# Fourth chunk of three later feed-forward parts by 7 products instead of 8, with its token sums formed at the head

## The chip, the cores and the metric

One core of one Trainium2 chip runs the whole kernel. The metric is the device time of one execution in microseconds (us), as the median of several runs. A profiled execution gives the trace from which all durations here are read.

## What is computed

Two layers of a hybrid block on 512 tokens of width 1024, in float32. Each layer is feed-forward, token mixing, feed-forward, with a layer norm behind each:

```python
def _swiglu(x, w1, w2):
    gt, up = jnp.split(x @ w1, 2, axis=-1)
    return (jax.nn.silu(gt) * up) @ w2

for l in range(DEPTH):          # DEPTH = 2, D_FF = 2816
    x = _layer_norm(DN_ALPHA * x + 0.5 * _swiglu(x, ffn1_w1[l], ffn1_w2[l]), ...)
    mix = _token_mix(x, ...)
    x = _layer_norm(DN_ALPHA * x + mix, ...)
    x = _layer_norm(DN_ALPHA * x + 0.5 * _swiglu(x, ffn2_w1[l], ffn2_w2[l]), ...)
```

So there are four feed-forward parts. This change concerns the products `x @ w1` of parts two, three and four.

## The kernel before

Every float32 operand is split into a high part, rounded to the type that TensorE multiplies (`hi`, `xh`, `th`; made by ScalarE), and the rest (`lo`, `xl`, `tl`; made by VectorE as operand minus high part). One product of two matrices is then three matmuls: high by high, high by rest, rest by high. Wherever below "product" stands for one 128x128 weight block against tokens, its three matmuls are counted singly.

A feed-forward part (`ffn`, L576) walks over 22 chunks of w1; chunk f is 128 gate columns and 128 up columns. There are two ways to do a chunk:

- Plain (`proj`, L186): gate and up, each 8 blocks of the inner dimension by 3 matmuls over all 512 tokens: 48 matmuls of 512 columns. With halves of weights and tokens as blocks of a 2 by 2 matrix these are 8 block products.
- By 7 products (`strassen`, L630, after Strassen and Winograd): 7 block products of 4 blocks by 3 matmuls over 256 tokens: 84 matmuls of 256 columns. It needs sums of the weights (`Pair.sums`, L522: four VectorE subtractions and additions into two `ws` tiles), the splits of `ug`, `u1`, `u2` and `ud` (`Pair.hi`, L532, high part on ScalarE, `lo` on VectorE at L544), and sums of the tokens (`token_sums`, L554: x put together from `xh` and `xl` in four VectorE instructions at L566, four subtractions at L570, split at L572 and L573 into `th` and `tl`). The token sums are formed once per part.

The head of a part runs in this order. Chunks 0 and 1 are done by `staged` (L464) with weights that the part before has loaded; each of their four results (`pj`) is done for 256 tokens first and for the other 256 behind. Their weights (`hi`, `lo`) lie in a pool `nx`, which is given back (`done_prev`, L685) when the matmuls have been issued. Then pools are opened in that memory: `fb` with `hb` (the last four chunks' results), `fa` with `ha` (one tile of 18 chunks' results, 36 KB in each partition, L691) and, on the other side of memory, `w1p` with the tiles for sums. These pools have `reuse_waits="tile"`: a tile in memory that was used before waits for those who used it before. Then `evac` (L584) makes silu(gate) times up of chunks 0 and 1, first ScalarE (L586, from PSUM to a place in `ha`), then VectorE (L587). Chunks 2 and 3 are plain. Beside them VectorE forms the token sums, evacuates chunk 2, and prepares chunk 4's weights. From chunk 4 to chunk 21 all are done by 7 products: `strassen(f, cur, ahead)` with the next chunk's sums and splits put between its products as `slots`.

In the last three parts TensorE, GpSimd, ScalarE and VectorE run their instructions in the order of the code (`in_order`, L256, entered at L681 since `l or which` holds). In the first part this begins at chunk 4 only. PSUM has eight banks, given in turn by a ring (`ps`, L81); a result tile waits until the bank's last user is done. Weight splits are put into pools in turn (`unit`, L144): a counter `more.n` picks the pool.

Names used below: `pj` results of chunks 0 and 1; `pg`, `pu` and `pv` results of gate, up and the third bank of a chunk; `ha` the tile of chunk results; `ws` sums of weights; `dl` the rest of `ud`.

Of the kernel before, what the change touches and what calls it, by code (L numbers as in the profile page):

```python
# [9 lines left out]
F32 = mybir.dt.float32  # L10
F32R = mybir.dt.float32r
BF = mybir.dt.bfloat16
AF = mybir.ActivationFunctionType
OP = mybir.AluOpType
# [4 lines left out]
P = 128  # L19
S, D, F = 512, 1024, 2816  # L20
KD, KF, NB = D // P, F // P, S // P
# [43 lines left out]
def body(tc, a, out, depth=DEPTH):  # L65
    nc = tc.nc
# [12 lines left out]
    ring = [0]  # L79

    def ps(tag=None, name="ps", shape=(P, 512)):  # L81
        if tag is None:
            tag = PS_ALL[ring[0] % 8]
            ring[0] += 1
        return psp.tile(list(shape), F32, name=name, tag=tag, bufs=PS_TAGS[tag])
# [22 lines left out]
    xh = xtp.tile([P, KD, S], F32R, name="xh")  # L108
    xl = xtp.tile([P, KD, S], F32R, name="xl")
# [16 lines left out]
    def wraw():  # L126
        pl, n = raws[0]
        raws.rotate(-1)
        return pl.tile([P, KD, P], F32, name="raw", tag="raw", bufs=n)

    more = K()
# [24 lines left out]
    def wsplit(raw, n=KD, step=None):  # L156
        hi, lo = unit()
        step = step or n
        for i in range(0, n, step):
            c = slice(i, i + step)  # L160
            nc.scalar.activation(hi[:, c], raw[:, c], AF.Copy)  # L161
            nc.vector.tensor_tensor(lo[:, c], raw[:, c], hi[:, c].bitcast(F32), op=OP.subtract)  # L162
        return hi, lo

    def wcols(w, c0, step=None):

        r = wraw()
        nc.sync.dma_start(r, w.rearrange("(k p) f -> p k f", p=P)[:, :, c0:c0 + P])
        return wsplit(r, step=step)
# [6 lines left out]
    def mm3(o, w, k, vh, vl, first, last):  # L176
        hi, lo = w
        if lo is None:
            nc.tensor.matmul(o[0:64], hi[:, k, 0:64], vh, start=first, stop=False)
            nc.tensor.matmul(o[0:64], hi[:, k, 0:64], vl, start=False, stop=last)  # L180
            return
        nc.tensor.matmul(o, hi[:, k], vh, start=first, stop=False)  # L182
        nc.tensor.matmul(o, hi[:, k], vl, start=False, stop=False)  # L183
        nc.tensor.matmul(o, lo[:, k], vh, start=False, stop=last)  # L184

    def proj(o, w, n=slice(0, S), ks=range(KD)):  # L186
        for k in ks:
            mm3(o[:, n], w, k, xh[:, k, n], xl[:, k, n], k == 0, k == KD - 1)
# [67 lines left out]
    def in_order():  # L256
        m = tc.manual_schedule(engines={PE, POOL, mybir.EngineType.Activation, mybir.EngineType.DVE})
        m.__enter__()
        return m
# [252 lines left out]
    class Pair:  # L512
# [34 lines left out]
        def all(u):  # L547
# [3 lines left out]
                u.hi(n)()  # L551
            return u

    def token_sums(st):  # L554


        x = st.ha[:, 10:18]
        th, tl = (st.w1p.tile([P, 4, 4, 256], F32R, name=n) for n in ("th", "tl"))
        t = [y[:, i:i + 2].rearrange("p a (b s) -> p (a b) s", b=2) for y, i in
             ((st.hb, 0), (st.hb, 2), (st.ha, 6), (st.ha, 8))]  # L560
        tt = nc.vector.tensor_tensor
        nc.gpsimd.tensor_copy(pace, st.ha[:, 0, 0:1])
        nc.gpsimd.memset(one, 1.0)
        for i in range(0, KD, 2):
            c = slice(i, i + 2)
            nc.vector.scalar_tensor_tensor(x[:, c], xh[:, c].bitcast(F32), one, xl[:, c].bitcast(F32), op0=OP.mult,  # L566
                                           op1=OP.add)
        p_, q, r_, s_ = x[:, 0:4, 0:256], x[:, 0:4, 256:512], x[:, 4:8, 0:256], x[:, 4:8, 256:512]
        for i, u, v in ((0, q, p_), (1, s_, t[0]), (2, s_, q), (3, r_, t[1])):
            tt(t[i], u, v, op=OP.subtract)  # L570
        for i in range(4):
            nc.scalar.activation(th[:, i], t[i], AF.Copy)  # L572
            tt(tl[:, i], t[i], th[:, i].bitcast(F32), op=OP.subtract)  # L573
        st.t = [(th[:, i], tl[:, i]) for i in range(4)]

    def ffn(l, w1, w2, which, xap, xa, wts, pend, done_prev, last, nxt, ts, mid=()):  # L576


        st = K()
# [4 lines left out]
        def evac(f, pg, pu, t=None):  # L584
            t = st.w1p.tile([P, S], F32, name="v", tag="v", bufs=2) if t is None else t
            nc.scalar.activation(t, pg, AF.Silu)  # L586
            nc.vector.tensor_tensor(hpart(f), t, pu, op=OP.mult)  # L587
# [3 lines left out]
        def parts(hi, lo, x):  # L591
            nc.scalar.activation(hi, x, AF.Copy)  # L592
            nc.vector.tensor_tensor(lo, x, hi.bitcast(F32), op=OP.subtract)
# [36 lines left out]
        def strassen(f, u, nxt_, slots=None):  # L630


            if slots is None:
                slots = [nxt_.sums, lambda: (nxt_.hi("ug")(), late.append(nxt_.hi("u1"))),
                         lambda: (late.pop()(), late.append(nxt_.hi("u2"))),
                         lambda: (late.pop()(), late.append(nxt_.hi("ud")))]
            late = []
            t1, t2, t3, t4 = st.t
            ga, pa, pb = ps(name="pg"), ps(name="pu"), ps(name="pv")
            p_, r_, s_ = [(xh[:, k:k + 4, c], xl[:, k:k + 4, c]) for k, c in ((0, H1), (4, H1), (4, H2))]  # L640

            def prod(o, w, k0, x, first=True):
                for k in range(4):
                    hi, lo = w[0][:, k0 + k], w[1][:, k0 + k]
                    vh, vl = x[0][:, k], x[1][:, k]
                    for i, (wx, vx) in enumerate(((hi, vh), (hi, vl), (lo, vh))):
                        nc.tensor.matmul(o, wx, vx, start=first and k == 0 and i == 0, stop=k == 3 and i == 2,  # L647
                                         skip_group_check=True)

            tt = nc.vector.tensor_tensor  # L650
            for g in st.tail:
                g()
            slots[0]()
            prod(ga[:, H1], u.ug, 0, p_)
            prod(ga[:, H2], u.u1, 0, t1, False)
            sn = st.w1p.tile([P, S], F32, name="sn", tag="sn", bufs=2)
            nc.scalar.activation(sn, ga, AF.Copy)
            slots[1]()
            prod(pa[:, H1], u.u1, 4, t2)
            prod(pa[:, H2], u.u2, 0, t3, False)  # L660
            v = st.w1p.tile([P, S], F32, name="v", tag="v", bufs=2)
            h = hpart(f)
            tt(v[:, H1], pa[:, H1], sn[:, H1], op=OP.add)
            tt(v[:, H2], pa[:, H2], v[:, H1], op=OP.add)
            tt(h[:, H2], sn[:, H2], v[:, H2], op=OP.add)
            slots[2]()
            prod(pb[:, H1], u.ud, 0, t4)
            tt(h[:, H1], pb[:, H1], v[:, H2], op=OP.add)
            slots[3]()
            prod(ga[:, H1], u.ug, 4, r_, False)  # L670
            prod(ga[:, H2], u.u2, 4, s_, False)

            def add():
                tt(ga[:, H2], ga[:, H2], v[:, H1], op=OP.add)

            def silu():
                nc.scalar.activation(v, ga, AF.Silu)

            st.tail = [add, silu] + late + [lambda: tt(h, v, h, op=OP.mult)]

        order = in_order() if l or which else None  # L681
        pts = staged(wts, pend, mid)
# [9 lines left out]
        st.w1p = nx.w1 = pool("w1p", side="right", reuse_waits="tile")  # L692
        more.n = 4
        more_raws(st.lnp, 1)
        ws = [(wcols(w1, f * P), wcols(w1, F + f * P)) for f in (2, 3)]
        for f in (2, 3):
            evac(f - 2, *pts[2 * f - 4:2 * f - 2], st.ha[:, f + 2])
        pps = []
        for w in ws:
            pps.append((ps(name="pg"), ps(name="pu")))  # L700
            for o, x in zip(pps[-1], w):
                proj(o, x)
        token_sums(st)
        evac(2, *pps[0])
        cur = Pair(w1, 4).all()
        evac(3, *pps[1])
        st.tail = []
        ahead = Pair(w1, 5)
        order = order or in_order()
        for f in range(4, KF):  # L710
            for i in range(2 if f % 3 == 0 else 1):
                sums_step(hpart(f - 2))
# [1 line left out]
            if f == KF - 1:  # L714
                w = [wt.tile([P, KD, P], F32R, name=n, tag=n, bufs=3).rearrange("p (a b) c -> p a (b c)", a=4)
                     for n in ("hi", "lo")]
                v, sn = (st.w1p.tile([P, 2, 256], F32, name=n, tag=n, bufs=2) for n in ("v", "sn"))
# [6 lines left out]
            cur, ahead = ahead, Pair(w1, f + 2) if f + 2 < KF else None  # L724
        v, sn = (st.w1p.tile([P, 2, 256], F32, name=n, tag=n, bufs=2) for n in ("v", "sn"))
        w = [st.w1p.tile([P, 4, 256], F32R, name="ws", tag="ws", bufs=2) for _ in range(2)]
# [5 lines left out]
        def lo(u, r):  # L732
            nc.vector.tensor_tensor(u[1], r, u[0].bitcast(F32), op=OP.subtract)
# [1105 lines left out]
    w = xl[:, KD - 1, 256:512].bitcast(BF)  # L1839
    nc.vector.memset(w, 1.0)  # L1840
    o = ps("po", "warm")
# [155 lines left out]
```

## Time and profile before

| | |
|---|---|
| median of 3 runs | 2423.96 us (2423.51 to 2423.97) |
| the profiled execution | 2423.59 us |
| its span, first to last instruction | 2421.9 us |
| TensorE (PE) busy | 2408.2 us, 99% |
| VectorE (DVE) busy | 1947.0 us, 80% |
| ScalarE (ACT) busy | 1228.6 us, 51% |
| GpSimd (POOL) busy | 488.2 us, 20% |

The profiled execution lies 1.7 us above its span; that rest lies outside the instructions. A row of the timeline gives start and length in us, the engine, the line of the code, the operation with what it writes and reads, and in brackets how long the engine was idle before it and for whom it waited. Matmuls overlap: a matmul's length is longer than the distance to the next one's start, and it is the distance that adds up. VectorE instructions overlap by some hundredths too.

### The profile page before, as it was taken

Reading aid. Unit: us, or ns where it says so; the run is one execution under the profiler, and the core shown is the slowest. Engines: PE = TensorE matmul, PEld = TensorE weight load, DVE = VectorE, ACT = ScalarE, POOL = GpSimd, SP = SyncE. Lnnn points to the kernel's source line nnn. Section 1 sums busy time; section 2 is a strip of 40 time slices with the busy share of each in tenths; the row PEclk is TensorE's granted clock in tenths of the full one; section 3 lists DMA queues with packets and bytes.
Section 4 is the critical chain, followed back from the end, with each engine's and each line's share of the span. In section 5 each row is a group of like instructions: output and inputs, shape, how many; then the busy total and the mean of one; then the engine's idle time right before and its main releaser. Section 6 shows DMA issues by size and latency. Waiting matters only on the chain.

```text
span 2421.9 us, 41995 instructions
## 1 busy us (share of the span) xinstructions
PE 2408.2 (99%) x15952; PEld 2156.7 (89%) x15952; DVE 1947.0 (80%) x3782; ACT 1228.6 (51%) x2336; POOL 488.2 (20%) x684
## 2 busy tenths in 40 slices
PE   9999999999999999999999999999999999999998
PEld 8999887888889889998899998878888898899987
DVE  6899985687688669999879999666776885799997
ACT  4444645577544334445544446455766443344463
POOL 4232402144410002114000004022443100000040
PEclk9999999999999999999999999999999999999999
DMA  7888754666483536887533347546765735233373
GB/s 208 228 224 216 258 154 138 175 158 157 118 196 96 188 100 166 210 210 243 184 106 105 105 131 250 153 134 168 164 145 119 195 105 183 79 104 106 106 240 121
DMA packets 422586, 390.09 MB, mean 161 GB/s; under 512 B 20472, under 2 KB 352392, under 8 KB 422384
## 3 DMA queue, kind: packets, MB, share of 16 engines
q1 hardware_dynamic: 385792, 287.00, 39.8%
q0 software_dynamic: 36592, 100.41, 17.3%
q8 instruction: 126, 2.06, 0.3%
q14 instruction: 76, 0.62, 0.1%
HBM read 360.02 MB, written 93.38 MB: 187 GB/s over the span
## 4 chain that ended last, share of the span: by engine, by line
PE 99%; DMA 0%; issue 0%; ACT 0%; DVE 0%; DVEq 0%; POOLq 0%; SPq 0%; POOL 0%; ACTq 0%
PE acc L331 18%; PE pg L647 17%; PE pu L647 9%; PE pj L182 6%; PE gate L1657 6%; PE pj L183 6%; PE pj L184 6%; PE pv L647 4%; PE brp L184 2%; PE brp L182 2%; PE brp L183 2%; PE sN L1258 2%; PE ptN L1300 1%; PE po L1319 1%; PE acc L197 1%; PE acc L196 1%
## 5 line engine op out<-in xcount | busy, mean ns | idle before, releaser
L162 DVE TENSOR_TENSOR lo<-raw,hi 128x1024 fp32r<-128x1024 f32 (+2 forms) x186 | 216.5, 1182 | 86.0 <-ACT hi L161 85.1
L182 PE MATMUL pj<-xh,hi 128*128 128x512 f32 (+1 forms) x720 | 267.2, 371 | 0.6 <-ACT hi L161 0.6
L184 PE MATMUL pj<-xh,lo 128*128 128x512 f32 (+1 forms) x720 | 254.7, 354 | 0.4 <-DVE lo L162 0.4
L183 PE MATMUL pj<-xl,hi 128*128 128x512 f32 (+1 forms) x720 | 254.6, 354 | 0.0
L161 ACT ACTIVATE hi<-raw 128x1024 fp32r<-128x1024 f32 (+2 forms) x186 | 185.9, 1019 | 130.6 <-PE acc L331 52.9
L647 PE MATMUL pg<-xh,lo 128*128 128x256 f32 x864 | 244.7, 283 | 0.0
L647 PE MATMUL pg<-xl,hi 128*128 128x256 f32 x864 | 244.7, 283 | 0.0
L647 PE MATMUL pg<-xh,hi 128*128 128x256 f32 x864 | 244.7, 283 | 0.0
L331 PE MATMUL acc<-hi,sh 128*128 128x512 f32 x568 | 221.6, 390 | 0.0
L331 PE MATMUL acc<-lo,sh 128*128 128x512 f32 x568 | 221.2, 389 | 0.0
L331 PE MATMUL acc<-hi,sl 128*128 128x512 f32 x568 | 221.1, 389 | 0.0
L352 POOL COPY pace<-sh 64x1 f32<-64x1 f32 x16 | 94.8, 5927 | 473.9 <-ACT sh L592 473.9
L544 DVE TENSOR_TENSOR lo<-ws,hi 128x1024 fp32r<-128x1024 f32 x144 | 175.2, 1217 | 0.0
L647 PEld LDWEIGHTS pg<-xl,hi 128*128 128x128 f32 x864 | 166.0, 192 | 0.2
L647 PEld LDWEIGHTS pg<-xh,hi 128*128 128x128 f32 x864 | 166.0, 192 | 0.2
L647 PEld LDWEIGHTS pg<-xh,lo 128*128 128x128 f32 x864 | 166.0, 192 | 0.0
L647 PE MATMUL pu<-tl,hi 128*128 128x256 f32 x576 | 163.1, 283 | 0.0
L647 PE MATMUL pu<-th,hi 128*128 128x256 f32 x576 | 163.1, 283 | 0.0
L647 PE MATMUL pu<-th,lo 128*128 128x256 f32 x576 | 163.1, 283 | 0.0
L184 PEld LDWEIGHTS pj<-xh,lo 128*128 128x128 f32 x720 | 136.2, 189 | 20.1 <-DVE lo L162 0.6
L541 ACT ACTIVATE hi<-ws 128x1024 fp32r<-128x1024 f32 x144 | 143.9, 1047 | 16.9 <-DVE ws L526 15.3
L182 PEld LDWEIGHTS pj<-xh,hi 128*128 128x128 f32 x720 | 136.5, 190 | 16.3 <-issue 3.7
(418 smaller groups left out, 7072.8 us busy)
## 6 DMA issues: line engine op xcount, KB each, us to landing
raw<-in_ffn_w_dram SPq DMA_DIRECT2D x228, 512.0 KB, 4.7
ts<-in_ffn_w_dram POOLq DMA_DIRECT2D x72, 768.0 KB, 7.3
raw<-in_w_in_dram SPq DMA_DIRECT2D x56, 512.0 KB, 4.0
raw<-ts SPq DMA_DIRECT2D x52, 512.0 KB, 4.1
raw<-in_w_gate_dram SPq DMA_DIRECT2D x48, 512.0 KB, 4.7
ts<-ts POOLq DMA_DIRECT2D x24, 768.0 KB, 8.5
x_sp<-xa POOLq DMA_DIRECT2D x24, 512.0 KB, 6.1
ks<-hl SPq DMA_DIRECT2D x96, 128.0 KB, 2.5
```

The source lines that it names most:

```text
L161: nc.scalar.activation(hi[:, c], raw[:, c], AF.Copy)
L162: nc.vector.tensor_tensor(lo[:, c], raw[:, c], hi[:, c].bitcast(F32), op=OP.subtract)
L182: nc.tensor.matmul(o, hi[:, k], vh, start=first, stop=False)
L183: nc.tensor.matmul(o, hi[:, k], vl, start=False, stop=False)
L184: nc.tensor.matmul(o, lo[:, k], vh, start=False, stop=last)
L331: nc.tensor.matmul(o, xx[:, t], ww[:, c], start=first and i == 0, stop=last and i == 2)
L352: nc.gpsimd.tensor_copy(pace[0:64], sp(min(p + 1, NS - 1))[0][0:64, 0, 0:1].bitcast(F32))
L541: nc.scalar.activation(t[0], x, AF.Copy)
L544: nc.vector.tensor_tensor(t[1], x, t[0].bitcast(F32), op=OP.subtract)
L647: nc.tensor.matmul(o, wx, vx, start=first and k == 0 and i == 0, stop=k == 3 and i == 2, skip_group_check=True)
L1258: nc.tensor.matmul(o[:, 0:nb].rearrange("p k b j -> p (k b j)"), q, kx[:, 2 * b0:2 * (b0 + nb)].rearrange("p a b -> p (a b)"), start=i == ...
L1657: nc.tensor.matmul(o, wx, vx, start=first and k == 0 and i == 0, stop=k == 3 and i == 2, skip_group_check=True)
```

## The change

Three edits go together:

1. In the last three parts chunk 3 is done by 7 products; chunks 0, 1 and 2 stay as they were. The new `token_sums_early` writes x into chunks 0 to 7 of `ha` and the sums into `hb` and chunks 8 to 11 of `ha`, with plain additions (it drops the GpSimd copy and memset, and the three-operand form, of `token_sums`). It stands ahead of the evacuation of chunks 0 and 1 (`first_two`), which moves behind all splits of chunk 3. The evacuation of chunk 2 is put at the front of `strassen(3, ...)`.
2. The PSUM ring skips four banks at the head of every part, the first included, so chunk 2 takes the banks of the last transposes instead of those of chunk 0.
3. `more.n -= 1`: chunk 3 now takes three weight units instead of two, and the counter is set back by one, so that later chunks take the pools that they took before.

The first part keeps its code but for the four banks.

```diff
+    def token_sums_early(st):
+        th, tl = (st.w1p.tile([P, 4, 4, 256], F32R, name=n) for n in ("th", "tl"))
+        x = st.ha[:, 0:8]
+        t = [y[:, i:i + 2].rearrange("p a (b s) -> p (a b) s", b=2) for y, i in
+             ((st.hb, 0), (st.hb, 2), (st.ha, 8), (st.ha, 10))]
+        tt = nc.vector.tensor_tensor
+        for i in range(0, KD, 2):
+            c = slice(i, i + 2)
+            tt(x[:, c], xh[:, c].bitcast(F32), xl[:, c].bitcast(F32), op=OP.add)
+        p_, q, r_, s_ = x[:, 0:4, 0:256], x[:, 0:4, 256:512], x[:, 4:8, 0:256], x[:, 4:8, 256:512]
+        for i, u, v in ((0, q, p_), (1, s_, t[0]), (2, s_, q), (3, r_, t[1])):
+            tt(t[i], u, v, op=OP.subtract)
+
+        def parts():
+            for i in range(4):
+                nc.scalar.activation(th[:, i], t[i], AF.Copy)
+                tt(tl[:, i], t[i], th[:, i].bitcast(F32), op=OP.subtract)
+            st.t = [(th[:, i], tl[:, i]) for i in range(4)]
+        return parts
...
-        ws = [(wcols(w1, f * P), wcols(w1, F + f * P)) for f in (2, 3)]
+        ws = [(wcols(w1, f * P), wcols(w1, F + f * P)) for f in ((2,) if order else (2, 3))]
+        ring[0] += 4
...
+        if order:
+            cur = Pair(w1, 3)
+            plain_pairs()
+            lo = cur.hi("ug")
+            parts_ = token_sums_early(st)
+            v2 = st.w1p.tile([P, S], F32, name="v", tag="v", bufs=2)
+            cur.sums()
+            lo()
+            parts_()
+            more.n -= 1
+            los = [cur.hi(n) for n in ("u1", "u2", "ud")]
+            for lo in los:
+                lo()
+            first_two()
+            st.tail = [lambda: evac(2, *pps[0], v2)]
+            ahead = Pair(w1, 4)
+            strassen(3, cur, ahead)
+            cur, ahead = ahead, Pair(w1, 5)
+        else:
+            first_two()
+            plain_pairs()
+            token_sums(st)
...
```

How the instructions move is shown at two places of the second part's head; the third and fourth parts have the same order. A semaphore named in brackets is what a row waits for (`PE_49` TensorE, `Activation_49` ScalarE, `Pool_49` GpSimd, `DMA...` a transfer); x2 stands for two equal rows.

VectorE, before, from the last weight split of chunk 3 to the first of chunk 4 (`lo<-raw,hi` at L162 is a plain chunk's split, `ha<-ha,pj` the evacuation of chunks 0 and 1, `ha<-xh,pace,xl` x put together, L570 the token sums, `ha<-v,pu` the evacuation of chunk 2):

```order
L162 TENSOR_TENSOR lo<-raw,hi 128x1024 [waits DMAHW1_49,Activation_49]
L587 TENSOR_TENSOR ha<-ha,pj 128x512 [waits Activation_49]
L587 TENSOR_TENSOR ha<-ha,pj 128x512 [waits PE_49,Activation_49]
L566 SCALAR_TENSOR_TENSOR ha<-xh,pace,xl 128x1024 [waits DVE_49,Pool_49]
L566 SCALAR_TENSOR_TENSOR ha<-xh,pace,xl 128x1024
L566 SCALAR_TENSOR_TENSOR ha<-xh,pace,xl 128x1024 [waits DVE_49]
L566 SCALAR_TENSOR_TENSOR ha<-xh,pace,xl 128x1024
L570 TENSOR_TENSOR hb<-ha 128x1024 [waits DVE_49]
```

VectorE, the same place after the change, from the sums of chunk 3's weights on (`L525` to `L528`; `L544` the rests of `ug`, `u1`, `u2` and `ud`, `L609` the evacuation). Ahead of these rows stand the splits of chunk 2, the four additions at L563, the first of which waits for TensorE, and the four token sums:

```order
L525 TENSOR_TENSOR ws<-raw 128x512 [waits DMAHW1_49]
L526 TENSOR_TENSOR ws<-ws,raw 128x512 [waits DMAHW0_49,DVE_49]
L527 TENSOR_TENSOR ws<-raw 128x512
L528 TENSOR_TENSOR ws<-raw,ws 128x512 [waits DVE_49]
L544 TENSOR_TENSOR lo<-raw,hi 128x1024 [waits Activation_49]
L571 TENSOR_TENSOR tl<-hb,th 128x1024 [waits Activation_49] x2
L571 TENSOR_TENSOR tl<-ha,th 128x1024 [waits Activation_49] x2
L544 TENSOR_TENSOR lo<-ws,hi 128x1024 [waits PE_49,Activation_49]
L544 TENSOR_TENSOR lo<-ws,hi 128x1024 [waits Activation_49]
L544 TENSOR_TENSOR dl<-raw,dh 128x512 [waits Activation_49]
L609 TENSOR_TENSOR ha<-ha,pj 128x512 [waits Activation_49] x2
L609 TENSOR_TENSOR ha<-v,pu 128x512 [waits PE_49,Activation_49]
```

The evacuation went from the front to the back of this stretch. The two plain splits of chunk 3 are gone, and the sums and splits of its weights stand where chunk 4's stood.

TensorE behind chunk 2, before (chunk 3, plain, with nothing waited for):

```order
L184 MATMUL pu<-xh,lo 128x512
L182 MATMUL pg<-xh,hi 128x512
L183 MATMUL pg<-xl,hi 128x512
L184 MATMUL pg<-xh,lo 128x512
L182 MATMUL pg<-xh,hi 128x512
```

TensorE behind chunk 2 after the change, from the tenth to the fifteenth matmul of chunk 3, where its first block product ends and the second, which reads the token sums, begins. The nine ahead of them are `pg<-xh,hi`, `pg<-xl,hi` and `pg<-xh,lo` three times, of which the very first waits for TensorE and ScalarE and the third for VectorE:

```order
L669 MATMUL pg<-xh,hi 128x256
L669 MATMUL pg<-xl,hi 128x256
L669 MATMUL pg<-xh,lo 128x256
L669 MATMUL pg<-th,hi 128x256 [waits Activation_49]
L669 MATMUL pg<-tl,hi 128x256 [waits DVE_49]
L669 MATMUL pg<-th,lo 128x256 [waits DVE_49]
```

Chunk 3 now waits for VectorE three times in its first 15 matmuls, where it waited for nothing: for the rest of `ug` at the third, for the token sums' rests at the 14th and for the rest of `u1` at the 15th.

More of the change, by code (lines that the diff above doesn't have):

```diff
@@ L694, in ffn, with plain_pairs, first_two @@
         more_raws(st.lnp, 1)
-        ws = [(wcols(w1, f * P), wcols(w1, F + f * P)) for f in (2, 3)]
-        for f in (2, 3):
-            evac(f - 2, *pts[2 * f - 4:2 * f - 2], st.ha[:, f + 2])
+        ws = [(wcols(w1, f * P), wcols(w1, F + f * P)) for f in ((2,) if order else (2, 3))]
+        ring[0] += 4
         pps = []
[L699 to L709, printed above, removed]
+        def plain_pairs():
+            for w in ws:
+                pps.append((ps(name="pg"), ps(name="pu")))
+                for o, x in zip(pps[-1], w):
+                    proj(o, x)
+        def first_two():
+            for f in (2, 3):
+                evac(f - 2, *pts[2 * f - 4:2 * f - 2], st.ha[:, f + 2])
+        if order:
[20 more added lines that the diff above has]
+            token_sums(st)
+            evac(2, *pps[0])
+            cur = Pair(w1, 4).all()
+            evac(3, *pps[1])
+            st.tail = []
+            ahead = Pair(w1, 5)
+            order = in_order()
         for f in range(4, KF):
```

## The prediction

> **What bounds the kernel now.** I read the page first: its span, busy shares and chain of waits.
>
> ```profile
> span 2421.9 us, 41995 instructions
> PE 2408.2 (99%) x15952; PEld 2156.7 (89%) x15952; DVE 1947.0 (80%) x3782; ACT 1228.6 (51%) x2336; POOL 488.2 (20%) x684
> ...
> PE 99%; DMA 0%; issue 0%; ACT 0%; DVE 0%; DVEq 0%; POOLq 0%; SPq 0%; POOL 0%; ACTq 0%
> ```
>
> TensorE is busy for 2408.2 of 2421.9 us and the chain stays on it. So any TensorE time taken out shortens the kernel, and any stall put in lengthens it, one for one. Next the waits of TensorE:
>
> ```profile
> PE hid L1030 <- DMA cw<-in_cmp_k_w_dram: 2.0, 2, 1.5
> ...
> PE pg L182 <- ACT ha L586: 1.1, 2, 0.6
> ```
>
> The longest wait behind the kernel's start is 1.5 us (second number: how often; third: the longest). The wait of chunk 2's first matmul for the evacuation happens twice, 0.6 us each; those are parts two and four.
>
> Next, how full each engine is where the change lies. The first three windows run from the first write into `ha` (I call this T0: 900.80, 1239.01 and 2102.63) to the first matmul of chunk 4; the fourth holds one later 7-product chunk, 84 matmuls.
>
> ```profile
> core 0: us, PE busy (x) PEld busy (x) DVE busy (x) ACT busy (x) POOL busy (x), PEclk, DMA share, GB/s
> 900.80:923.34 22.54, 21.97 (x97) 18.14 (x97) 21.84 (x23) 9.90 (x12) 2.58 (x4) 1.00 0.12 36
> 1239.01:1260.60 21.59, 21.59 (x96) 17.84 (x95) 20.89 (x22) 9.21 (x11) 0.21 (x2) 1.00 0.01 2
> 2102.63:2125.17 22.54, 21.97 (x97) 18.14 (x97) 21.84 (x23) 9.90 (x12) 0.21 (x2) 1.00 0.05 13
> 936.29:946.37 10.08, 10.08 (x86) 10.08 (x85) 9.32 (x15) 4.67 (x6) 3.06 (x5) 1.00 0.98 227
> ```
>
> This is the view that matters. Here VectorE is as full as TensorE: 21.84 of 22.54 us. It has just finished chunk 4's preparation when TensorE wants it. Two plain chunks are the cover of that work, and the change takes one of them away.
>
> **TensorE's own gain.** The timeline of TensorE at the second part:
>
> ```profile
> 886.25 0.36 PE L182 MATMUL pj<-xh,hi 128*128 128x256 f32 x1
> ...
> 900.48 0.28 PE L183 MATMUL pj<-xl,hi 128*128 128x256 f32 x1
> ...
> 901.45 0.50 PE L182 MATMUL pg<-xh,hi 128*128 128x512 f32 x1 [0.57 <-ACT ha L586]
> ...
> 912.46 0.39 PE L182 MATMUL pg<-xh,hi 128*128 128x512 f32 x1
> ...
> 923.34 0.28 PE L647 MATMUL pg<-xh,hi 128*128 128x256 f32 x1
> ```
>
> A plain chunk takes 923.34 − 912.46 = 10.88 us for 48 matmuls (0.227 each), a 7-product chunk 10.08 for 84 (0.12 each). So 0.80 us a part go, 2.4 in all. The bank skip removes the wait of 0.57 us in parts two and four, 1.1 us. The bank that chunk 2 now takes was last used by the transposes, done ahead of 886.25, so nothing is late in its place there. In the first part its wait doesn't exist, so I cost it at nothing. Together TensorE could give 3.5 us, and about 0.6 more from the exact start of chunk 2.
>
> [...]
>
> **What VectorE must do first, and from when.** The evacuation is what the diff moves away, so I looked at when `ha` is written first (ScalarE's timeline, part two):
>
> ```profile
> 900.80 1.09 ACT L586 ACTIVATE ha<-pj 128x512 f32<-128x512 f32 x2 [8.53 <-PE pj L183]
> ```
>
> ScalarE sat idle for 8.53 us. Its first operand `pj` was ready long before: 24 matmuls from 886.25 on, 886.25 + 24 × 0.12 = 889.1. What it waited for was the matmul that starts at 900.48, the last but one of `staged`. The reason I read from it: `ha` is one tile of 36 KB that lies over the weights of chunks 0 and 1, and under `reuse_waits="tile"` its first writer waits for the last reader of those weights. The change puts another first writer there, the addition at L563, and in the changed program that row waits for TensorE; counting the semaphore through the program, its value is reached by the same last-but-one matmul (in part three the last one). Chunks 0 to 7 of `ha` may lie in memory that is long free; the wait is by tile. VectorE's chain still begins at T0, and what stood ahead of it, the evacuation, was short.
>
> VectorE's timeline gives the length of each step:
>
> ```profile
> 888.16 4.63 DVE L162 TENSOR_TENSOR lo<-raw,hi 128x1024 fp32r<-128x1024 f32 x4
> ...
> 902.63 4.87 DVE L566 SCALAR_TENSOR_TENSOR ha<-xh,pace,xl 128x1024 f32<-128x1024 f32 x4
> 907.42 1.22 DVE L570 TENSOR_TENSOR hb<-ha 128x1024 f32<-128x1024 f32 x1
> ...
> 912.09 2.35 DVE L573 TENSOR_TENSOR tl<-hb,th 128x1024 fp32r<-128x1024 f32 x2
> 914.36 2.36 DVE L573 TENSOR_TENSOR tl<-ha,th 128x1024 fp32r<-128x1024 f32 x2
> 916.62 0.68 DVE L587 TENSOR_TENSOR ha<-v,pu 128x512 f32<-128x512 f32 x1
> 917.22 1.22 DVE L544 TENSOR_TENSOR lo<-raw,hi 128x1024 fp32r<-128x1024 f32 x1
> 918.36 0.69 DVE L525 TENSOR_TENSOR ws<-raw 128x512 f32<-128x512 f32 x1
> ...
> 920.90 2.43 DVE L544 TENSOR_TENSOR lo<-ws,hi 128x1024 fp32r<-128x1024 f32 x2
> ```
>
> Starts to starts. The four additions: a plain addition of this shape isn't in the trace; the nearest row is the plain subtraction at 888.16, four in 4.63 with the last one's tail, so 4.54; the three-operand form took 907.42 − 902.63 = 4.79, the upper bound. Token sums: 912.09 − 907.42 = 4.67. Weight sums: 920.90 − 918.36 = 2.54. The rest of `ug`: 1.22. They end at T0 + 4.54 + 4.67 + 2.54 + 1.22 = T0 + 12.97. Then the token sums' rests, 916.62 − 912.09 = 4.53 behind a start at T0 + 12.89, and the rest of `u1`, 1.22: T0 + 18.64.
>
> TensorE, without its wait, starts chunk 2 at about 900.72 and chunk 3 at T0 + 10.8. Two matmuls later it needs the rest of `ug`: it stalls from T0 + 11.0 to 13.0, **2.0 us**. Twelve matmuls (1.45 us) later, at the 15th, it needs the rest of `u1`, which in VectorE's order stands behind all four rests of the token sums: it stalls from T0 + 14.4 to 18.6, **4.2 us**. The rests of `u2` and `ud` follow on VectorE 1.2 and 1.8 us later, the matmuls that read them 24 × 0.12 = 2.9 and 36 × 0.12 = 4.3 us later, so they are in time. The remaining 70 matmuls take 8.40, and chunk 4 starts at T0 + 18.64 + 8.40, with some hundredths for the handing over **T0 + 27.1**.
>
> Against the trace of before: 900.80 + 27.1 = 927.9 for 923.34, 4.56 us later; part three 1266.11 for 1260.60, 5.51 later; part four 2129.73 for 2125.17, 4.56 later. Sum 14.63 us.
>
> **The rest of the edits.** The moved evacuation now ends behind the rest of `ud`, and the third bank of chunk 3 waits for ScalarE's part of it; ScalarE is half idle (9.90 of 22.54), and that bank is needed 34 matmuls behind the stall, so nothing. The dropped copy and memset on GpSimd and the pool counter cost nothing on a path: GpSimd is busy for 0.21 to 2.58 us there, and later chunks find the pools as before. Chunk 4's preparation now lies beside chunk 3's matmuls, behind the moved evacuation. Its rest of `u1` comes at T0 + 28.3, by the lengths above, against a need at T0 + 27.1 + 14 × 0.12 = 28.8: 0.5 us of margin. The loads:
>
> ```profile
> raw<-in_ffn_w_dram SPq DMA_DIRECT2D x228, 512.0 KB, 4.7
> ```
>
> Chunk 5's raw weights are loaded where chunk 3's were, free at about T0 + 13 (gate) and T0 + 20.4 (up); 4.7 us later is T0 + 25.1, and they are needed at about T0 + 31.
>
> **Rivals.** *The memory is free by place.* If the additions don't wait for `staged`, VectorE starts at 888.16 + 2 × 1.14 = 890.4, 10.4 us ahead of T0, the rest of `u1` is there at T0 + 8.3, and nothing stalls. Chunk 4 starts at T0 + 10.8 + 10.08 = T0 + 20.9, in part three T0 + 20.8: 1.66 + 0.80 + 1.66 = 4.1 us gained, 2419.5. It decides as soon as the additions start 8.2 us ahead of T0. For it: the operands are there, and those weights fill only some chunks of `ha`. Against it: the 8.53 us that ScalarE waited for another's memory, and the wait counted in the changed program. Chance 0.07.
>
> *TensorE's clock falls in the stall.* No wait of before is as long as 4.2 us, so nothing shows whether TensorE comes back at full speed. At its first work it did not run at it:
>
> ```profile
> 1.92 2.76 PE L1843 MATMUL warm<-xl 128*128 128x512 bf16 x6
> 4.69 1.09 PE L1932 MATMUL xT<-ident,xa 128*128 128x128 f32 x4
> 5.94 1.89 PE L1932 MATMUL xT<-ident,xa 128*128 128x128 f32 x12 [0.16 <-DMA xa<-in_x_dram]
> ...
> 885.46 1.04 PE L251 MATMUL pt<-ident,xa 128*128 128x128 f32 x8
> ```
>
> Four transposes took 1.09 us where later eight take 1.04, so half rate; from 5.94 on twelve took 1.89, near full. So it ran slow for about 5.94 − 1.92 = 4.0 us. As much behind each stall costs half of that, 2.0 us: 2440.2 if it hits one head, 2444.2 if all three. [...] I give all three heads, or two with a longer slow stretch, 0.14; one head stays in the forecast's case.
>
> *Chunk 4 is late too.* If its margin of 0.5 us fails, by 1 us in each head, the time is 2441.2. Chance 0.07.
>
> **How the numbers follow.** 2423.59 (the profiled execution; 0.4 below the median) + 14.6 = 2438.2, chance 0.72. Low end: 1 us off each head, about one VectorE instruction of 1024 elements less on the chain, 2435. High end: the slow clock in all three heads, 2444.5; the slower additions (0.75 in all), chunk 4 being late and one slow head lie inside. The range leaves out the free memory and the upper half of the slow clock. A measurement of this kernel can tell about 0.2%, 4.8 us, from no change. The free memory's 4.1 us lie just within it: faster 0.02, same 0.05, slower 0.93.
>
> **What would show it.** Right: in chunk 3 of each of three parts TensorE waits at its third matmul about 2.0 us for `lo` and at its 15th about 4.2 us for `lo`, VectorE's first addition starts at the end of `staged` after an idle time of some 10 us, and chunk 2's wait for ScalarE is gone. Wrong: the additions start right behind the splits of chunk 2; or the 15th matmul waits for something other than VectorE; or the 70 matmuls behind it take clearly over 8.4 us (the clock).

## The result and the profile after

The changed kernel takes 2443.45 us (median of 6 runs, 2442.22 to 2444.07) where the kernel before takes 2423.94: a ratio of 1.0079, 95% interval 1.0069 to 1.0089. It is slower by 19.5 us. The forecast was 2438.2 us, its range 2435.0 to 2444.5. The profiled execution took 2444.07 us, 20.5 us more than that of before. Of all executions reported here one was of another kind: one of the twelve of the last version below took 10097.64 us, for which nothing here gives a reason, and it is left out of that version's ratio.

The page and TensorE's waits of the changed kernel (in total, how often, the longest):

```profile
span 2442.4 us, 42241 instructions
PE 2416.0 (99%) x16060; PEld 2168.6 (89%) x16060; DVE 1964.8 (80%) x3815; ACT 1236.6 (51%) x2345; POOL 487.7 (20%) x678
...
PE 97%; DVE 2%; issue 1%; DMA 0%; ACT 0%; DVEq 0%; POOLq 0%; SPq 0%; POOL 0%; ACTq 0%
```

```profile
PE pg L669 <- DVE lo L544: 15.1, 6, 3.5
...
PE hid L1079 <- DMA cw<-in_cmp_k_w_dram: 0.8, 2, 0.4
```

VectorE now stands in the chain with 2%, and TensorE waits for it six times, 15.1 us in all: twice in chunk 3 of each of three parts. The wait of chunk 2 for ScalarE is gone. But waits of 15.1 us, with the 4.1 us against them that the plain chunk and the wait of chunk 2 give back, do not make 20.5. TensorE's busy time has risen as well, from 2408.2 to 2416.0, although chunk 3 should take less of it. The timeline of TensorE at part two's head tells why:

```profile
911.38 0.28 PE L669 MATMUL pg<-xh,hi 128*128 128x256 f32 x1
911.50 0.28 PE L669 MATMUL pg<-xl,hi 128*128 128x256 f32 x1
913.58 0.39 PE L669 MATMUL pg<-xh,lo 128*128 128x256 f32 x1 [1.80 <-DVE lo L544]
...
914.39 0.29 PE L669 MATMUL pg<-xh,lo 128*128 128x256 f32 x1
914.51 0.39 PE L669 MATMUL pg<-xh,hi 128*128 128x256 f32 x1
914.70 0.41 PE L669 MATMUL pg<-xl,hi 128*128 128x256 f32 x1
...
915.13 0.41 PE L669 MATMUL pg<-th,hi 128*128 128x256 f32 x1
915.34 0.41 PE L669 MATMUL pg<-tl,hi 128*128 128x256 f32 x1
919.25 0.58 PE L669 MATMUL pg<-th,lo 128*128 128x256 f32 x1 [3.50 <-DVE lo L544]
919.63 0.41 PE L669 MATMUL pg<-th,hi 128*128 128x256 f32 x1
919.85 0.41 PE L669 MATMUL pg<-tl,hi 128*128 128x256 f32 x1
...
930.15 0.28 PE L669 MATMUL pg<-xh,hi 128*128 128x256 f32 x1
```

The two forecast waits are there, at the third and the 15th matmul, both for `lo`. But from the tenth matmul on, at 914.51, matmuls start 0.21 us apart instead of 0.12, and the 70 matmuls behind the second wait take 930.15 − 919.25 = 10.90 us, not 8.40. The windows of that stretch give the granted clock (the column behind POOL):

```profile
911.60:913.60 2.00, 0.20 (x3) 0.03 (x1) 2.00 (x4) 1.93 (x3) 0.00 (x0) 1.00 0.00 0
913.60:914.50 0.90, 0.90 (x7) 0.90 (x8) 0.90 (x1) 0.88 (x2) 0.00 (x0) 1.00 0.00 0
914.50:915.50 1.00, 1.00 (x7) 0.96 (x5) 1.00 (x2) 0.99 (x2) 0.00 (x0) 0.52 0.61 171
915.50:919.20 3.70, 0.26 (x2) 0.00 (x0) 3.70 (x5) 1.39 (x3) 0.00 (x0) 0.50 0.32 95
919.20:921.90 2.70, 2.65 (x12) 2.65 (x13) 2.70 (x4) 0.11 (x1) 0.00 (x0) 0.50 0.00 0
921.90:924.60 2.70, 2.70 (x15) 2.70 (x14) 2.67 (x6) 1.95 (x3) 1.30 (x2) 0.50 0.66 194
...
926.60:930.15 3.55, 3.55 (x31) 3.55 (x31) 3.48 (x6) 0.63 (x1) 0.00 (x0) 1.00 0.74 216
```

The clock is halved from 914.5 to about 924.7, through the second wait, and this happened after a first wait of only 1.80 us. In the trace's record of the granted clock the fall lies at 914.53 and the return at 924.77, 10.24 us later; parts three and four show the same, for 10.24 us each (from 1259.28 and from 2129.68). This is the profiled execution, the slowest of the six. Its mean granted clock is 0.993; that of the five others is 0.994 to 0.997, for 0.999 in the profiled execution of before, so the clock was down for a part of them too, in some for a shorter time.

VectorE's timeline at the same place:

```profile
900.55 4.63 DVE L563 TENSOR_TENSOR ha<-xh,xl 128x1024 f32<-128x1024 f32 x4 [10.28 <-PE pj L183]
...
912.30 1.22 DVE L544 TENSOR_TENSOR lo<-raw,hi 128x1024 fp32r<-128x1024 f32 x1
...
917.98 2.35 DVE L544 TENSOR_TENSOR lo<-ws,hi 128x1024 fp32r<-128x1024 f32 x2
```

VectorE stood idle for 10.28 us ahead of its first addition, waiting for TensorE's `pj`. The rest of `ug` ended at 912.30 + 1.22 = T0 + 12.97 and the rest of `u1` at 917.98 + 1.22 = T0 + 18.65, both as worked out.

For comparing kernels one length serves: from the first matmul of `staged` behind the transposes (886.25 in part two before) to the first of chunk 4 (923.34). The starts come from the timelines; they read 37.09, 36.26 and 37.09 us in parts two, three and four before, and 44.15, 44.04 and 43.90 now. The sum is 110.44 before and 132.09 now: 21.65 us lost at the three heads. Around them 1.2 us were won that the forecast did not have: part two's head begins 0.24 us earlier, and the stretch from part three's chunk 4 to part four's head is 0.93 us shorter. The two waits of `hid` for a transfer, one in each of these stretches, fell from 2.0 to 0.8 us in all. 21.65 − 1.2 = 20.5.

### The profile page after: what moved, and what is told of

Read it like the earlier page. It is cut to its first block, busy times and chain, and to the rows that moved or that the text cites. A ratio compares the mean times of both kernels' runs of the same rounds, so it can differ in the third digit from the quotient of the medians.

```text
span 2442.4 us, 42241 instructions
## 1 busy us (share of the span) xinstructions
PE 2416.0 (99%) x16060; PEld 2168.6 (89%) x16060; DVE 1964.8 (80%) x3815; ACT 1236.6 (51%) x2345; POOL 487.7 (20%) x678
## 4 chain that ended last, share of the span: by engine, by line
PE 97%; DVE 2%; issue 1%; DMA 0%; ACT 0%; DVEq 0%; POOLq 0%; SPq 0%; POOL 0%; ACTq 0%
PE pg L669 18%; PE acc L331 17%; PE pu L669 9%; PE pj L182 6%; PE gate L1706 6%; PE pj L183 6%; PE pj L184 6%; PE pv L669 4%; PE brp L184 2%; PE brp L182 2%; PE brp L183 2%; PE sN L1307 2%; PE ptN L1349 1%; PE po L1368 1%; PE acc L197 1%; PE acc L195 1%
## 5 line engine op out<-in xcount | busy, mean ns | idle before, releaser
L162 DVE TENSOR_TENSOR lo<-raw,hi 128x1024 fp32r<-128x1024 f32 (+2 forms) x180 | 210.3, 1185 | 84.6 <-ACT hi L161 83.8
L669 PE MATMUL pg<-xh,lo 128*128 128x256 f32 x900 | 255.9, 284 | 5.5 <-DVE lo L544 5.5
L669 PE MATMUL pg<-xl,hi 128*128 128x256 f32 x900 | 255.5, 284 | 0.0
L669 PE MATMUL pg<-xh,hi 128*128 128x256 f32 x900 | 255.3, 284 | 0.0
L544 DVE TENSOR_TENSOR lo<-ws,hi 128x1024 fp32r<-128x1024 f32 x150 | 182.2, 1216 | 0.0
L669 PEld LDWEIGHTS pg<-xh,lo 128*128 128x128 f32 x900 | 173.7, 193 | 6.1 <-DVE lo L544 6.1
L669 PEld LDWEIGHTS pg<-xl,hi 128*128 128x128 f32 x900 | 173.5, 193 | 0.2
L669 PEld LDWEIGHTS pg<-xh,hi 128*128 128x128 f32 x900 | 173.3, 193 | 0.2
L669 PE MATMUL pu<-th,hi 128*128 128x256 f32 x600 | 171.6, 286 | 0.0
L669 PE MATMUL pu<-tl,hi 128*128 128x256 f32 x600 | 171.5, 286 | 0.0
L669 PE MATMUL pu<-th,lo 128*128 128x256 f32 x600 | 171.5, 286 | 0.0
```

The lines of the kernel that those rows point to most:

```text
L544: nc.vector.tensor_tensor(t[1], x, t[0].bitcast(F32), op=OP.subtract)
```

## The experiments

**Free memory by two tiles.** The theory: the additions wait because the tile-wide wait ties chunks 0 to 7 of `ha` to the weights under its other chunks.

```diff
-        st.ha = fa.tile([P, NA, S], F32, name="ha")
+        if order:
+            st.ha = Two(fa.tile([P, 12, S], F32, name="ha"), fa.tile([P, NA - 12, S], F32, name="hz"), 12)
+        else:
+            st.ha = fa.tile([P, NA, S], F32, name="ha")
```

(`Two` only passes an index on to the tile that holds it.)

> The chunk results of the last three parts lie in two tiles, chunks 0 to 11 and chunks 12 to 17, at the same addresses as the one tile; only the second lies over the weights of chunks 0 and 1. My theory (the additions wait because the wait is by tile): VectorE's first addition starts right behind the splits of chunk 2, some 10 us earlier (at about 890.4 in part two), TensorE has no wait in chunk 3, the granted clock stays at 1.00 there, and the kernel takes about 2419.4 us, 4 to 4.5 us less than before and 24 us less than the changed kernel. Rival (the additions are held by something else, or TensorE waits in chunk 3 for another reason): start and stalls stay as they are, 2443 us.

Measured: 2426.93 us, ratio 1.0013 (1.0005 to 1.0022). In part two VectorE's first addition starts behind the second split of chunk 2, with no idle time; in part three it still waits:

```profile
888.48 2.36 DVE L162 TENSOR_TENSOR lo<-raw,hi 128x1024 fp32r<-128x1024 f32 x2
890.75 4.62 DVE L579 TENSOR_TENSOR ha<-xh,xl 128x1024 f32<-128x1024 f32 x4
```

```profile
1237.69 3.50 DVE L579 TENSOR_TENSOR ha<-xh,xl 128x1024 f32<-128x1024 f32 x3 [10.40 <-PE pj L184]
```

TensorE's waits of this kernel:

```profile
PE pg L685 <- DVE lo L544: 5.9, 2, 4.0
```

Only two of six waits are left, both in part three. The heads take 35.45, 43.18 and 35.45 us: parts two and four are 1.64 us shorter than before, as in the forecast's first rival. The expectation failed for part three. The memory map of the program (no trace shows it) gives the reason: in part three the weights of chunks 0 and 1 lie from the start of `ha` on, under its chunks 0 to 15, so the first of the two tiles is not free either; in parts two and four they lie under its last chunks, 14 to 17. Parts two and four show that the wait goes by the tile and where it lies; part three shows that "free" differs from part to part.

**Another order on VectorE and ScalarE.** One tile and its wait stay; the weight sums and the rest of `ug` move ahead of the additions, and the splits of the weights (high part on ScalarE, rest on VectorE) go between those of the token sums.

```diff
+            th, tl = (st.w1p.tile([P, 4, 4, 256], F32R, name=n) for n in ("th", "tl"))
+            v2 = st.w1p.tile([P, S], F32, name="v", tag="v", bufs=2)
             lo = cur.hi("ug")
-            parts_ = token_sums_early(st)
-            v2 = st.w1p.tile([P, S], F32, name="v", tag="v", bufs=2)
             cur.sums()
             lo()
-            parts_()
+            parts_ = token_sums_early(st, th, tl)
             more.n -= 1
-            los = [cur.hi(n) for n in ("u1", "u2", "ud")]
-            for lo in los:
-                lo()
+            for i, n in enumerate(("u1", "u2", "ud")):
+                parts_(i)
+                cur.hi(n)()
+            parts_(3)
```

> The one tile stays, and VectorE still waits for the end of the chunks 0 and 1. Only the order on VectorE and ScalarE changes: the weight sums of chunk 3 and the rest of ug come ahead of the first addition (in its 10 us of idle time), and the rests of u1, u2 and ud are put between those of the token sums. My theory (the length of VectorE's chain behind that wait, against one plain chunk of 10.8 us, is what TensorE waits for): chunk 3 has stalls of 0 to 0.3 us in all; chunk 4 then starts 6 to 9 us earlier than in the changed kernel, and its own rests come late by about 1 us at its third and 1 us at its 15th matmul, since VectorE has done nothing of chunk 4 by then. 2424 to 2428 us, up to 2431 if these short stalls bring the clock down too. Rival (the weights or their loads are late, not the chain): the waits stay and the time is above 2438.

Measured: 2425.72 us, ratio 1.0007 (0.9997 to 1.0016). TensorE's waits:

```profile
PE pg L667 <- DVE lo L544: 4.4, 6, 0.8
```

The heads take 35.62, 35.74 and 35.61 us, 0.2 to 0.3 above the 35.45 us of a head without any wait, so chunk 3 waits for next to nothing; the six waits lie in chunk 4, 0.7 us each on the mean (4.4 in all). The clock falls nowhere behind them (in part two it is 1.00 in every window from 915.00 to 930.70). The chain theory holds, and so does its cost: what VectorE no longer owes at chunk 3 it owes at chunk 4. All three heads were cured by the order of the same work on VectorE and ScalarE, which also shows that weights and loads were in time.

**Dummy matmuls in the waits.** Matmuls into a bank that the next product overwrites keep TensorE busy while it waits (`more` of them ahead of the third matmul of a block product):

```diff
+                        if k == 0 and i == 2:
+                            for j in range(more):
+                                nc.tensor.matmul(pa[:, H1], u.ug[0][:, 0], p_[0][:, 0], start=True, stop=True,
+                                                 skip_group_check=True)
...
-            prod(ga[:, H1], u.ug, 0, p_)
-            prod(ga[:, H2], u.u1, 0, t1, False)
+            prod(ga[:, H1], u.ug, 0, p_, True, fill[0])
+            prod(ga[:, H2], u.u1, 0, t1, False, fill[1])
...
-            strassen(3, cur, ahead)
+            strassen(3, cur, ahead, None, {(0, 2): (15, 33), (1, 0): (16, 0), (1, 2): (0, 14)}[l, which])
```

> Dummy matmuls of 256 columns, into a bank that the next product overwrites, stand in the stalls of chunk 3: in part two 15 ahead of the third matmul and 33 ahead of the 15th (both stalls filled), in part three 16 ahead of the third alone, in part four 14 ahead of the 15th alone. Theory of the clock (TensorE's clock is halved because it stood idle): in part two all matmuls of 256 columns start 0.12 us apart and chunk 4 starts about 4.3 us later than before, not 6.8; in part three the clock falls, if at all, only behind the second stall; in part four it falls behind the first stall of 1.8 us as it did. In all 2437.5 to 2441 us. Rival (the slow matmuls behind the stalls come from reading data that VectorE or ScalarE is just writing, or from contention in memory, not from idleness): part two has the same slow stretch of 10 us, and the time is 2443 us or more.

Measured: 2440.4 us, ratio 1.0067 (1.0054 to 1.0081). Windows: part two from chunk 3's start on, and part three behind its only wait:

```profile
911.40:919.30 7.90, 7.90 (x65) 7.62 (x63) 7.90 (x9) 5.50 (x7) 0.00 (x0) 1.00 0.22 66
919.30:926.50 7.20, 7.17 (x60) 6.97 (x59) 7.17 (x11) 3.48 (x4) 1.30 (x2) 1.00 0.44 125
1262.90:1266.30 3.40, 3.40 (x18) 3.40 (x17) 3.40 (x6) 1.55 (x2) 0.00 (x0) 0.50 0.27 80
```

With both waits filled the clock stays at 1.00 and the head takes 41.74 us, not 44.15, while VectorE and ScalarE work as before; so the slow matmuls come from TensorE's idle time, not from what the other engines do. Part three, with the second wait alone, is slow for 3.4 us; its head takes 43.35 us, 1.50 more than with both waits filled (41.85, below). Part four came out in another way than expected: the first wait, 1.80 us long as in the changed kernel, did not bring the clock down this time, the second did. The last section shows where the difference lies. Then all three heads filled:

```diff
-            strassen(3, cur, ahead, None, {(0, 2): (15, 33), (1, 0): (16, 0), (1, 2): (0, 14)}[l, which])
+            strassen(3, cur, ahead, None, (15, 30))
```

> As the kernel with dummy matmuls before, but in all three parts 15 of them ahead of the third matmul of chunk 3 and 30 ahead of the 15th, so that TensorE stands idle for at most 0.6 us at once. Theory (14.6 us of the loss are waits for VectorE, the other 7 the halved clock behind them): no matmul of 256 columns takes 0.21 us in chunk 3, chunk 4 starts at T0 + 27.1 in all three parts, 4.3 to 4.6 us later than before in parts two and four and 5.5 in part three, and the kernel takes 2436.5 to 2438 us. Rival (the waits alone make more than 14.6 us): 2440 us or more.

Measured: 2437.74 us, ratio 1.0055 (1.0042 to 1.0068), within what was expected. TensorE's waits, and the windows behind the second wait in the three parts:

```profile
PE pg L673 <- DVE lo L544: 1.2, 3, 0.4
```

```profile
919.80:926.40 6.60, 6.60 (x56) 6.60 (x57) 6.57 (x10) 3.31 (x4) 1.29 (x2) 1.00 0.46 133
...
1262.70:1269.20 6.50, 6.50 (x55) 6.50 (x56) 6.46 (x10) 3.24 (x4) 0.00 (x0) 1.00 0.29 83
...
2131.00:2137.50 6.50, 6.50 (x56) 6.50 (x56) 6.46 (x10) 3.26 (x4) 0.00 (x0) 1.00 0.27 81
```

The heads take 41.74, 41.85 and 41.74 us, 125.33 in all: 14.89 more than before, where the forecast's sum had 14.63. The other 6.76 us of the changed kernel's profiled execution (132.09 − 125.33) are the clock's.

**A doubled cost.** Each of the four additions stands twice.

```diff
-            tt(x[:, c], xh[:, c].bitcast(F32), xl[:, c].bitcast(F32), op=OP.add)
+            for _ in range(2):
+                tt(x[:, c], xh[:, c].bitcast(F32), xl[:, c].bitcast(F32), op=OP.add)
```

> The changed kernel with each of the four additions done twice, 4 more VectorE instructions of 1.135 us in each of three parts. Theory (the length of VectorE's chain behind the wait sets when chunk 3 goes on): the wait at the third matmul grows by 4.5 us in each part, and the time by 3 x 4.5 = 13.6 us, to 2457 us, a little less if the clock is low for a shorter part of the work. Rival (something else ends last there, or VectorE has slack): less than 5 us more.

Measured: 2459.06 us, ratio 1.0143 (1.013 to 1.0156), 15.6 us above the changed kernel; the profiled executions are 14.7 apart. TensorE's waits, and VectorE's additions and first token sum in part two:

```profile
PE pg L670 <- DVE lo L544: 28.9, 6, 7.0
```

```profile
900.40 9.67 DVE L564 TENSOR_TENSOR ha<-xh,xl 128x1024 f32<-128x1024 f32 x8 [10.28 <-PE pj L183]
909.99 1.22 DVE L567 TENSOR_TENSOR hb<-ha 128x1024 f32<-128x1024 f32 x1
```

The eight additions take 909.99 − 900.40 = 9.59 us, the four of the changed kernel 4.55: 5.04 more, where 4.5 were expected. The wait at the third matmul grows by as much, 5.03 us in each part (6.83, 6.96 and 6.84 us for 1.80, 1.92 and 1.80), so VectorE's chain had no slack at all. The wait at the 15th shrank to 2.75 us in each part (from 3.50, 3.07 and 3.02), which fits twelve matmuls at the halved clock between the two waits: an estimate from 3.98 us, the second wait where these matmuls ran at full clock (part three of the kernel with two tiles), gives 3.98 − 12 × 0.09 = 2.9. So the waits grow by 13.8 us in all (28.9 − 15.1) and the time by 14.7, and that the first lies so near the expected 13.6 is luck: two errors cancel. The time came out 2.1 us above the expected 2457. The heads take 49.24, 48.40 and 49.33 us, 14.9 more than in the changed kernel.

**The banks alone**, on the kernel before:

```diff
+        ring[0] += 4
         pps = []
```

> The kernel before with the skip of four banks alone. My theory (chunk 2's first matmul waited for a bank that ScalarE evacuated, 0.57 us in parts two and four): these two waits are gone, nothing else waits, 1.1 us less than before, 2422.8 us. Rival (the wait is hidden or comes back at another bank): 2423.9 us, with a new wait of about 0.6 us elsewhere.

Measured: 2422.28 us, ratio 0.9993 (0.9985 to 1.0002). The ratio alone does not tell this from no change. The trace does; two of TensorE's waits:

```profile
PE gate L182 <- ACT g L1463: 1.1, 1, 1.1
PE hid L1031 <- DMA cw<-in_cmp_k_w_dram: 0.9, 2, 0.5
```

Chunk 2's wait is gone, and the heads take 36.26 us in all three parts, 0.83 less in parts two and four, 1.66 in all. A new wait stands in the token mixing (`gate` for ScalarE, 1.1 us), and the wait of `hid` is 0.9 for 2.0; what ties these two to the banks stays open.

**A version from these results.** Two tiles and 7 products for chunk 3 in parts two and four; part three plain, as before; the bank skip everywhere. The main line (the split of the tile and the choice of plain chunks ask for `which` as well):

```diff
-        if order:
+        if which:
             cur = Pair(w1, 3)
```

> Two tiles for the chunk results and chunk 3 by 7 products in parts two and four alone, where chunks 0 to 11 lie in free memory; part three is as it was before the change but for the skip of four banks. Theory: no wait of TensorE and no low clock at any of the three heads; beside the kernel with the bank skip alone (2422.3 us) 0.8 us less in each of two parts, 2420.7 us, 3.2 us less than before. Rival (the gain is eaten by chunk 4 or 5, whose preparation has less cover): 2422.3 us or more, with a wait of TensorE in these chunks.

Measured: 2420.86 us, ratio 0.9986 (0.9977 to 0.9995), 3.2 us less than the 2424.09 of before beside it. No wait of TensorE at the heads is left, and they take 35.45, 36.26 and 35.45 us: 3.28 less than before in all, 1.66 of it from the bank skip and 1.62 from two 7-product chunks. It is faster than both kernels, by little: 0.14% for the kernel before. A free place for part three's x and sums would be worth another 0.8 us by an estimate from these heads (36.26 − 35.45); it wasn't tried.

**How long a wait brings the clock down.** Since a wait of 1.80 us had done it, two kernels left idle times of different length at the second wait, by fewer dummy matmuls (the first wait filled). The first of them has this line, the second 18, 13 and 9 for 24, 21 and 15:

```diff
-            strassen(3, cur, ahead, None, (15, 30))
+            strassen(3, cur, ahead, None, {(0, 2): (15, 24), (1, 0): (15, 21), (1, 2): (15, 15)}[l, which])
```

> The kernel with dummy matmuls, the first stall filled in all three parts, the second filled but for about 1.2 us (part two), 1.5 us (part three) and 2.2 us (part four). Reading A (the clock is set at the ends of windows of 3.4 us that run by themselves, and halves when TensorE stood idle for more than half of one): no fall in parts two and three; in part four a fall, some 2 chances in 3, that lasts 3.4 us. Reading B (only a window that is idle throughout halves it): no fall in any. Reading C (any idle time of a microsecond or so does): a fall in all three. 2437 to 2440 us.

> The same with about 1.9 us (part two), 2.5 us (part three) and 3.0 us (part four) left idle at the second stall. Reading A (more than half of a window of 3.4 us): a fall in part two in about 1 case of 3, in part three in about 4 of 5, in part four nearly surely, each 3.4 us long. Reading B (a whole idle window of 3.4 us): no fall in any. Reading C (any idle time of a microsecond or so): a fall in all three. 2437 to 2441 us.

Measured, in one execution each, with 2425.51 us for the kernel before beside them: 2437.3 and 2442.18 us, the second 1.2 us above what was expected; its heads take 43.23, 43.34 and 43.21 us, 1.5 more each than with all waits filled. The windows of the first, the idle stretch and what follows, in part four (its longest):

```profile
2128.20:2130.40 2.20, 0.05 (x1) 0.06 (x1) 2.20 (x3) 0.00 (x0) 0.00 (x0) 1.00 0.00 0
2130.40:2137.00 6.60, 6.60 (x55) 6.60 (x56) 6.57 (x10) 3.22 (x4) 0.00 (x0) 1.00 0.29 82
```

The windows of the second, in parts two, three and four:

```profile
917.50:919.50 2.00, 0.17 (x3) 0.05 (x1) 2.00 (x3) 0.00 (x0) 0.00 (x0) 1.00 0.00 0
920.15:923.55 3.40, 3.40 (x19) 3.40 (x18) 3.38 (x6) 1.55 (x2) 0.56 (x2) 0.51 0.35 98
923.55:927.00 3.45, 3.45 (x30) 3.45 (x30) 3.40 (x6) 2.43 (x3) 0.74 (x2) 0.99 0.79 246
...
1265.00:1268.40 3.40, 3.40 (x18) 3.40 (x17) 3.37 (x6) 1.55 (x2) 0.00 (x0) 0.51 0.50 144
...
2135.30:2138.70 3.40, 3.40 (x19) 3.40 (x18) 3.37 (x7) 1.60 (x3) 0.00 (x0) 0.50 0.52 154
```

No fall in the first kernel (waits of about 1.1, 1.4 and 2.2 us), a fall in all three parts of the second (about 1.8, 2.4 and 2.9 us), each for 3.4 us. A wait of 2.2 us that did nothing and one of 1.8 that did can't be told apart by length: where it lies must count. Reading B falls, since no idle time here reached 3.4 us; so does reading C. Windows that run by themselves (reading A) fit both kernels, but its limit of half a window is a little too low: the window of the first kernel in part four held 1.77 us of idle time, 52%, and the clock stayed up (last section).

## Why the prediction was right, and what it had wrong

- **The bound.** Right: stretches where VectorE is as full as TensorE can't give up a plain chunk's cover. VectorE's time of 12.97 and 18.65 us behind T0 came out to the hundredth, from rows of the kernel before; so close a match is more than such a sum can promise.
- **The start of the chain at T0.** Right, for the reason given: 10.28 us of idle time ahead of the first addition, gone in parts two and four once the tile was split. One number on the way is wrong: the evacuation's first operand was ready at 886.25 + 48 × 0.12 = 892.0, not 889.1, since the first 24 of these matmuls belong to another result. 892.0 is still 8.8 us ahead of T0, so the argument stands.
- **The two waits.** Right in place and, counted as the forecast counts them, in size. The trace counts the first, 1.80 to 1.92 us for 2.0, from the end of the matmul ahead; from the start that the third matmul would have had it is 913.58 − 911.62 = 1.96. The second is 3.0 to 3.5 us for 4.2, because the matmuls ahead of it already ran slowly and arrived later: where they ran at full clock (part three of the kernel with two tiles and of the first with dummy matmuls) it is 3.98 and 3.99. With the clock kept up, the heads lose 14.89 us against 14.63.
- **The size that was off: the clock.** The forecast gave the slow clock in all three heads a chance of 0.14 and 2.0 us each, and set the likeliest time without it, 5.25 us below the measured one. It fell in all three, for 6.76 us in all, 2.25 each, and one of the forecast's own signs of being wrong came true: the 70 matmuls behind the second wait took 10.90, 10.68 and 10.65 us for 8.40. Its chance, the author's estimate, was the step that was off, and the reason for that chance doesn't hold: the prediction says that nothing in the trace of before shows what a wait of 4.2 us does, but that trace has a fall at its end. The last matmul ends at 2414.24, and 2.30 us later the clock is halved:

```profile
2414.00:2416.50 2.50, 0.23 (x2) 0.00 (x0) 2.23 (x6) 1.20 (x2) 0.00 (x0) 1.00 0.43 159
2416.55:2421.80 5.25, 0.00 (x0) 0.00 (x0) 1.42 (x2) 0.00 (x0) 0.74 (x2) 0.50 0.27 100
```

The forecast looked at the wait of 4.2 us, while behind the first one of 1.80 us the clock already fell, at 914.53. That its price of 2.0 us came near is luck. It assumed some 4.0 slow us behind the second wait, and found them from the kernel's start; in fact the fall came at the first wait and lasted 10.24 us, of which 4.9 to 5.5 lie behind the second. A fall by the second wait alone costs 1.5 us (part three of the first kernel with dummy matmuls). The time lies in the stated range because its high end was set for this case. Ahead of the fall at 914.53 TensorE did not stand idle throughout: of the 3.41 us from 911.12 on it was idle for 1.80.
- **What was not in the sum.** 1.2 us won around the heads, seen also in the kernel with the banks alone in part (`hid` 0.9 for 2.0 us). The pool counter was not run alone; no wait points to it.
- **Chunk 4 late.** It wasn't: no wait of TensorE stands in chunk 4 of the changed kernel. There the slow clock gave VectorE more time (in part two chunk 4 starts 44.15 us into the head, for 41.74 with all waits filled); but with all waits filled, where chunk 4 starts at T0 + 27.2 (27.1 were forecast), it doesn't wait either.
- **Memory free by place.** As a rival for the time it was wrong, and as a mechanism it was half there: the place is free in two of three parts, but the wait of the one tile hid that.

## What to carry to other kernels

Before work is taken from one engine, look at how full the others are in that very stretch, and from which moment on they may begin: here the one tile, which in parts two and four touched busy memory only with its far end, waited as a whole (10.28 us of VectorE's idle time in part two, none with two tiles). Two smaller tiles, or an order that puts what is free to run into the idle time, gave back 16 to 18 of the 19.5 us here, though neither alone came below the kernel before. And TensorE's short waits had a second price behind them here, 1.5 us for a fall of the clock by one wait and 2.25 on the mean for two waits close together; dummy matmuls kept it away (granted clock 1.00) where the wait itself stayed. Whether a kernel's trace already shows a fall of the clock is to be read up to its very end.

## What the runs showed of the hardware

In three traces the granted clock changed at instants that lie whole multiples of one length apart. In that of the changed kernel it fell at 914.53, 1259.28 and 2129.68 us, for 10.24 us each time. The falls lie 344.75 and 870.40 us apart: 101.00 and 255.00 times 3.4133 us, a third of 10.24. In the kernel with the longer idle times the trace's record of the clock has the three falls at 920.19, 1264.93 and 2135.33 us, each 3.41 us long. They lie 344.75 and 1215.15 us apart: 101.00 and 356.00 such lengths. In the trace of before two changes of the clock, at 6.73 and 2416.54 us, lie 706.00 such lengths apart. These instants fit windows of 3.41 us that run by themselves through the kernel.

The rows below are such windows, laid through a trace from one of its changes of the clock. The idle time that a window held is its length less PE's busy time:

```profile
911.12:914.53 3.41, 1.61 (x12) 1.33 (x11) 3.41 (x5) 3.15 (x4) 0.00 (x0) 1.00 0.00 0
...
1249.20:1252.61 3.41, 1.70 (x12) 1.50 (x12) 3.41 (x4) 3.33 (x6) 0.00 (x0) 1.00 0.21 61
...
2126.52:2129.94 3.42, 1.65 (x14) 1.45 (x13) 3.42 (x4) 1.46 (x3) 0.00 (x0) 1.00 0.34 101
...
2148.32:2151.73 3.41, 2.40 (x11) 2.40 (x12) 3.41 (x5) 0.00 (x0) 0.00 (x0) 0.50 0.03 7
```

The first row is part two of the changed kernel: 1.80 us idle, and the clock fell at its end. Of the falls at the heads this is the least idle time. The second is part three of the kernel with two tiles, 1.71 us, and the third part four of the kernel with the shorter idle times, 1.77: there the clock stayed up. Part four of the first kernel with dummy matmuls belongs to these: a window's end at 2126.46 cut its first wait of 1.80 us, and the window held 1.69 of it. So at the heads of these runs 1.77 us of idle time in 3.41 left the clock up and 1.80 brought it down, a little over half. The ends of matmuls are modelled, so the limit is less sharp than these two numbers.

Coming back took more work here than staying up. The windows of the second and third row held 50% and 48% of work, and the clock stayed up. The fourth row is part four of the kernel with the doubled additions: the window held 70% of work, and the clock stayed down for one window more. So it did in part two of the changed kernel behind one with 62% (2.11 of 3.42 us, 917.94 to 921.36). In part three of the kernel with two tiles a window with 89% brought it back (3.05 of 3.42 us, 1256.02 to 1259.44).

One fall doesn't fit: in the kernel with another order the clock fell at 10.13 us, behind a window with 1.61 us of idle time, 0.9 us of transposes and 0.9 us of other matmuls. So the limit is shown for the matmuls of the heads alone, and on few cases.
